# A 3x3 convolution with row transforms: outputs over the pair's own input, and all loads ahead of all stores

## The chip, the cores and the metric

The kernel runs on one core of one Trainium2 chip. The metric is device time in microseconds of one execution; lower is better. The core has five engines with instruction streams of their own: TensorE (PE, with weight loads shown as PEld), VectorE (DVE), ScalarE (ACT), GpSimd (POOL) and SyncE (SP), which here only issues transfers. Transfers between HBM and the on-chip memory SBUF run on 16 DMA engines; matrix products land in PSUM.

## The reference

`x` is 16 images of 64 channels of 64 x 64, `weight` is 128 x 64 x 3 x 3, all float32. Each output is the sum over 64 input channels and nine taps of a zero-padded 3 x 3 convolution:

```
x_pad = np.pad(x, ((0, 0), (0, 0), (1, 1), (1, 1)), mode='constant')
output[b, co] += weight[co, ci, kh, kw] * x_pad[b, ci, kh:kh+h, kw:kw+w]
```

The output has 16 x 128 x 64 x 64 float32, 33.55 MB; the input 16.8 MB and the weights 0.3 MB.

## The kernel before, in words

**Tiling.** Two images make a pair: their 2 x 64 channels fill the 128 partitions, and there are eight pairs. One image plane of 64 x 64 float32 per partition, 2.1 MB over 128 partitions, is a *home*. The tile `homes` has nine of them. `X_HOME` says in which home the input of each pair lands, `O_HOME` in which two neighbouring homes its output is made (two images of 128 output channels, so an output takes two homes). Homes are used again: the inputs of pairs 5, 6 and 7 go where earlier inputs were.

**Work on a half.** Each pair is worked in two halves of 32 output rows. In each half 16 rows (F block) are made with a Winograd-like row transform and 16 rows (G block) with shared products, each 2 x 8 row pairs. GpSimd makes three float16 tiles from the input: `sums` (L106, tile `ss`), `diffs` (L113, `dd`) and `outers` (L119, `ee`); ScalarE makes a fourth, the cast `xh` (L124). In the first half of pair 0 VectorE does GpSimd's part. The transforms of half n + 2 are recorded ahead of the work on half n. TensorE then multiplies (L162) with seven prepared weight matrices into four PSUM accumulators, which are all of PSUM that there is: `pf1`, `pg1`, `pf2`, `pg2`. After a first round, `pf1`, `pg1` and `pf2` hold products that two output rows share. ScalarE copies each to SBUF (`copied`, L182, tiles `ux`, `ug`, `uy` from a pool of four), and TensorE adds a second round onto the same accumulators. The output rows are then sums: VectorE's L231 (`pg2 + ug`), L232 (`pf1 + uy`) and L233 (`ux - pf2`), and ScalarE's copy of `pg1` (L234). All four write rows of every second row of the pair's output homes.

**Order.** `keep` fixes the order on each engine as written. ScalarE's order in a half is: three copies, the cast for the next half, the copy of `pg1`. A half issues 54 products on TensorE.

**Transfers.** At the start SyncE issues the weights (L58), pair 0 in two parts, pairs 1 and 2 (L63), and pairs 3 and 4 in one transfer of 4 MB (L72). `NEXT_LOADS` issues the inputs of pairs 5, 6 and 7 after the first halves of pairs 2, 3 and 4, so they stand between stores on SyncE and wait until the home is free. `store` writes a pair in one transfer of 4 MB where the pair is in `BOTH` (L192), else in two of 2 MB (L201). Pair 0's store is issued on ScalarE's queue (q10 in the profile), all else on SyncE's (q1). `FEW` cuts the second store of pair 5: its last seven rows go as 124 partitions and 4 partitions, beside 128 partitions for the rows ahead.

Of the kernel before, what the change touches and what calls it, by code (L numbers as in the profile page):

```python
# [8 lines left out]
F32 = mybir.dt.float32  # L9
F16 = mybir.dt.float16  # L10
# [5 lines left out]
def kernel(  # L16
# [12 lines left out]
    nc = tc.nc  # L29
    B, CI, H, W = x.shape  # L30
    CO = weight.shape[0]
    assert H == 64 and W == 64 and CI == 64 and CO == 128 and B == 16
    NP = B // 2
    RB = 8

    keep = tc.keep_in_program_order
    x_rows = x.rearrange("b c h w -> (b c) h w")
    w_flat = weight.rearrange("co ci kh kw -> co (ci kh kw)")

    const = ctx.enter_context(tc.tile_pool(name="const", bufs=1))  # L40
    psum = ctx.enter_context(tc.tile_pool(name="psum", bufs=4, space=bass.MemoryType.PSUM))
    slots = ctx.enter_context(tc.tile_pool(name="slots", bufs=1))
    tpool = ctx.enter_context(tc.tile_pool(name="tpool", bufs=4))
    cpool = ctx.enter_context(tc.tile_pool(name="cpool", bufs=3))
    upool = ctx.enter_context(tc.tile_pool(name="upool", bufs=4))

    X_HOME = [0, 1, 2, 7, 8, 2, 7, 8]
    O_HOME = [5, 3, 0, 5, 3, 0, 5, 2]  # L50
    BOTH = (0, 3, 6)
    FEW = 5, 1, 7
    NEXT_LOADS = {(2, 0): 5, (3, 0): 6, (4, 0): 7}
    homes = slots.tile([128, 9, H, W], F32)
    xs = [homes[:, k, :, :] for k in X_HOME]

    w_raw = const.tile([CO, CI * 9], F32)
    keep(nc.sync.dma_start(w_raw, w_flat))  # L58

    def load(p, cuts=((0, H),)):  # L60
        for lo, hi in cuts:
            keep(
                nc.sync.dma_start(  # L63
                    xs[p][:, lo:hi, :], x_rows[128 * p : 128 * p + 128, lo:hi, :]
                )
            )

    load(0, ((0, 34), (34, H)))
    load(1)
    load(2)  # L70
    rows = x_rows[128 * 3 : 128 * 5, :, :].rearrange("(g p) h w -> p g h w", g=2)
    keep(nc.sync.dma_start(homes[:, 7:9, :, :], rows))  # L72

    ident = const.tile([128, 128], F16)
    make_identity(nc, ident)

    w16 = const.tile([CO, 2, CI * 9], F16)
    keep(nc.gpsimd.tensor_copy(w16[:, 0, :], w_raw))  # L78
    keep(nc.scalar.copy(w16[:, 1, :], w_raw))  # L79

    G0, G1, G2, G21, G01, HP, HM = range(7)
    Wt = const.tile([128, 7, 3, CO], F16)
    g0h = const.tile([128, 3 * CO], F32)
    th = const.tile([128, 3 * CO], F32)

    def wrow(i):
        return Wt[:, i, :, :].rearrange("p t c -> p (t c)")
# [10 lines left out]
    F_BLK, G_BLK = (1, 2), (0, 3)  # L98
# [10 lines left out]
    def diffs(eng, p, h):  # L109
# [3 lines left out]
        keep(eng.tensor_sub(t, v[:, j : j + RB, 1, :], v[:, j : j + RB, 0, :]))  # L113
        return t

    def outers(eng, p, h):
        t = tpool.tile([128, 16, W], F16, tag="ee", name="ee")
        r = 16 * F_BLK[h]
        keep(eng.tensor_sub(t, xs[p][:, r - 1 : r + 15, :], xs[p][:, r + 1 : r + 17, :]))  # L119
        return t  # L120

    def cast(p, h):
        t = cpool.tile([128, 17, W], F16, tag="xh", name="xh")
        keep(nc.scalar.copy(t, xs[p][:, C_ROW[h] : C_ROW[h] + 17, :]))  # L124
        return t

    def transforms(eng, p, h):
        return sums(eng, p, h), diffs(eng, p, h), outers(eng, p, h)
# [12 lines left out]
    keep(nc.scalar.copy(wrow(G2), wps[2]))  # L141
    keep(nc.vector.tensor_sub(wrow(G21), wps[2], wrow(G1)))
    tr[0, 0] = s0, d0, outers(nc.vector, 0, 0)
    tr[0, 1] = transforms(nc.gpsimd, 0, 1)

    def mms(tiles, terms, start, stop):
        n = 3 * len(terms)
        i = 0
        for wi, src, row in terms:
            for kw in (1, 0, 2):  # L150
                c_lo, c_hi = max(0, 1 - kw), min(W, W + 1 - kw)
                lo, hi = 0, RB
                at, step, rows = row
                while at + step * lo < 0:
                    lo += 1
                while at + step * (hi - 1) > rows - 1:
                    hi -= 1
                first, last = at + step * lo, at + step * (hi - 1)
                for b2 in range(2):
                    p0 = 64 * b2  # L160
                    keep(
                        nc.tensor.matmul(  # L162
                            tiles[:, b2, lo:hi, c_lo:c_hi],
                            Wt[p0 : p0 + 64, wi, kw, :],
                            src[
                                p0 : p0 + 64,
                                first : last + 1 : step,
                                c_lo + kw - 1 : c_hi + kw - 1,
                            ],
                            start=start and i == 0,  # L170
                            stop=stop and i == n - 1,
                            skip_group_check=not start,
                        )
                    )
                i += 1

    def acc():
        return psum.tile([128, 2, RB, W], F32, tag="acc", name="acc")

    def copied(tiles):  # L180
        ut = upool.tile([128, 2, RB, W], F32, tag="ut", name="ut")
        keep(nc.scalar.copy(ut, tiles))  # L182
        return ut

    halves = [(p, h) for p in range(NP) for h in range(2)]

    def store(p, both):
        if p in BOTH:
            pair = out[2 * p : 2 * p + 2, :, :, :].rearrange("b c h w -> c b h w")

            eng = nc.scalar if p == 0 else nc.sync
            keep(eng.dma_start(pair, both))  # L192
            return
        for b2 in range(2):
            parts = [(0, CO, 0, H)]
            if (p, b2) == FEW[:2]:
                at = H - FEW[2]
                parts = [(0, CO, 0, at), (0, 124, at, H), (124, 4, at, H)]
            for c, n, lo, hi in parts:
                keep(  # L200
                    nc.sync.dma_start(  # L201
                        out[2 * p + b2, c : c + n, lo:hi, :], both[c : c + n, b2, lo:hi, :]
                    )
                )

    for n, (p, h) in enumerate(halves):
        if n + 2 < len(halves):
            tr[halves[n + 2]] = transforms(nc.gpsimd, *halves[n + 2])
        if h == 0:
            both = homes[:, O_HOME[p] : O_HOME[p] + 2, :, :]  # L210
            ov = both.rearrange("p b (j i) c -> p b j i c", i=2)
        ss, dd, ee = tr.pop((p, h))
        xc = xh.pop((p, h))
        jf, jg = RB * F_BLK[h], RB * G_BLK[h]
        sf, sg = jf - 16 * h, jg - 16 * h
        g_at = 2 * jg - C_ROW[h]

        pf1, pg1, pf2, pg2 = acc(), acc(), acc(), acc()
        mms(pf1, [(HP, ss, (sf, 1, 16))], True, True)
        ux = copied(pf1)  # L220
        mms(pg1, [(G1, ss, (sg, 1, 16))], True, True)
        ug = copied(pg1)
        mms(pf2, [(HM, dd, (0, 1, RB))], True, True)
        uy = copied(pf2)
        if n + 1 < len(halves):
            xh[halves[n + 1]] = cast(*halves[n + 1])
        mms(pg2, [(G01, xc, (g_at, 2, 17)), (G2, xc, (g_at + 2, 2, 17))], True, True)
        mms(pf1, [(G0, ee, (0, 2, 16))], False, True)
        mms(pg1, [(G21, xc, (g_at + 1, 2, 17)), (G0, xc, (g_at - 1, 2, 17))], False, True)
        mms(pf2, [(G2, ee, (1, 2, 16))], False, True)  # L230
        keep(nc.vector.tensor_add(ov[:, :, jg : jg + RB, 1, :], pg2, ug))  # L231
        keep(nc.vector.tensor_add(ov[:, :, jf : jf + RB, 0, :], pf1, uy))  # L232
        keep(nc.vector.tensor_sub(ov[:, :, jf : jf + RB, 1, :], ux, pf2))  # L233
        keep(nc.scalar.copy(ov[:, :, jg : jg + RB, 0, :], pg1))  # L234
        if h == 1:
            store(p, both)
        if (p, h) in NEXT_LOADS:
            load(NEXT_LOADS[p, h])


# [28 lines left out]
```

## Time and profile before

| what | value |
|---|---|
| median of the three runs shown | 126.89 us (126.59 to 128.24) |
| the profiled execution's own time | 126.95 us |
| its span, first to last instruction | 125.2 us |
| TensorE busy | 95.7 us, 76% |
| GpSimd busy | 90.5 us, 72% |
| ScalarE busy | 81.4 us, 65% |
| VectorE busy | 63.9 us, 51% |
| read from HBM / written | 17.07 MB / 33.55 MB |

The page cuts the span into 40 slices and shows each engine's busy share of a slice in tenths. The row DMA is the mean busy share of the 16 DMA engines, GB/s what they moved. In rows such as `102.66 1.22 DVE homes L233` the columns are start, duration, engine, tile and line. In rows of groups, `x48 | 45.7, 1020 | 6.3 <-PE` is the count, then the busy time in us and the mean ns of one, then the idle time ahead of them and what ended it. In a table of stretches each row has the stretch, its length, the busy time and count of each engine, the granted TensorE clock, the DMA share and GB/s. SPq and ACTq are the issuing sides of SyncE and ScalarE.

### The profile page before, as it was taken

How to read it: one execution, taken by the hardware profiler on the slowest of the kernel's cores; microseconds unless marked ns; L12 is line 12 of the kernel's file. 1: busy time of each engine (PE TensorE's matmuls, PEld its weight loads, DVE VectorE, ACT ScalarE, POOL GpSimd, SP SyncE). 2: the span in 40 equal slices, each digit the busy share in tenths (PEclk: the TensorE clock that was granted, in tenths of full speed). 3: DMA queues.
4: the chain of work that ended last, by engine and by line, in shares of the span. 5: the costliest groups of instructions: out<-in, count | busy, mean ns of one | idle time of the engine just before them, and what ended most of it. 6: DMA issues, size and time to landing. Idle time of an engine off the chain costs nothing.

```text
span 125.2 us, 2157 instructions
## 1 busy us (share of the span) xinstructions
PE 95.7 (76%) x873; PEld 50.5 (40%) x873; DVE 63.9 (51%) x56; ACT 81.4 (65%) x86; POOL 90.5 (72%) x52
## 2 busy tenths in 40 slices
PE   0349999999999999999999999999999980000000
PEld 0224455455555555555555555555555530000000
DVE  0199657374939375674839393746647392000000
ACT  4457598599797978889897979788897940000000
POOL 2209999999999999999999999999999400000000
PEclk9999999999999999999999999999999997555555
DMA  4999999999999999999999999999999999999981
GB/s 125 375 454 424 429 429 429 435 335 419 424 429 435 435 419 429 403 437 440 437 411 382 440 424 419 429 440 424 435 419 431 426 414 436 429 440 435 419 372 58
DMA packets 3826, 50.77 MB, mean 406 GB/s; under 512 B 360, under 2 KB 488, under 8 KB 744
## 3 DMA queue, kind: packets, MB, share of 16 engines
q1 hardware_dynamic: 3544, 46.43, 88.6%
q10 hardware_dynamic: 272, 4.19, 7.9%
q8 instruction: 7, 0.11, 0.3%
q14 instruction: 3, 0.02, 0.0%
HBM read 17.07 MB, written 33.55 MB: 405 GB/s over the span
## 4 chain that ended last, share of the span: by engine, by line
PE 76%; DVE 3%; DMA 2%; POOL 1%; ACT 0%; issue 0%; DVEq 0%
PE acc L162 76%; DMA w_raw<-in_weight_dram 2%; DVE homes L233 1%; DVE ss L106 1%; POOL w L78 1%; DVE th L133 0%; DVE Wt L134 0%; PE wp L95 0%; ACT g0h L131 0%; DVEq L134 0%
## 5 line engine op out<-in xcount | busy, mean ns | idle before, releaser
L162 PEld LDWEIGHTS <-Wt 64*128 64x128 f16 x864 | 49.6, 96 | 47.0 <-issue 3.7
L182 ACT COPY ut<-acc 128x1024 f32<-128x1024 f32 x48 | 45.7, 1020 | 6.3 <-PE acc L162 6.3
L162 PE MATMUL acc<-xh,Wt 64*128 64x504 f16 (+3 forms) x384 | 46.3, 372 | 0.0
L106 POOL TENSOR_TENSOR ss<-homes 128x1024 f16<-128x1024 f32 x15 | 35.5, 2369 | 4.7 <-DMA homes<-in_x_dram 4.7
L231 DVE TENSOR_TENSOR homes<-acc,ut 128x1024 f32<-128x1024 f32 x16 | 19.6, 1225 | 32.2 <-PE acc L162 29.7
L119 POOL TENSOR_TENSOR ee<-homes 128x1024 f16<-128x1024 f32 x15 | 35.6, 2375 | 0.0
L162 PE MATMUL acc<-ss,Wt 64*128 64x504 f16 (+1 forms) x192 | 24.9, 392 | 2.3 <-DVE ss L106 2.3
L162 PE MATMUL acc<-ee,Wt 64*128 64x504 f16 (+1 forms) x192 | 26.5, 377 | 0.0
L234 ACT COPY homes<-acc 128x1024 f32<-128x1024 f32 x16 | 16.2, 1015 | 11.3 <-PE acc L162 10.7
L233 DVE TENSOR_TENSOR homes<-ut,acc 128x1024 f32<-128x1024 f32 x16 | 19.5, 1220 | 2.0 <-PE acc L162 1.4
L113 POOL TENSOR_TENSOR dd<-homes 128x512 f16<-128x512 f32 x15 | 20.2, 1347 | 0.0
L232 DVE TENSOR_TENSOR homes<-acc,ut 128x1024 f32<-128x1024 f32 x16 | 19.4, 1215 | 0.0
L124 ACT CAST xh<-homes 128x1088 f16<-128x1088 f32 x16 | 17.9, 1120 | 0.0
L162 PE MATMUL acc<-dd,Wt 64*128 64x504 f16 (+1 forms) x96 | 13.9, 392 | 0.0
L95 PE MATMUL wp<-ident,w 128*128 128x128 f16 x9 | 1.1, 309 | 4.6 <-POOL w L78 4.6
L133 DVE SCALAR_TENSOR_TENSOR th<-wp,g0h 128x384 f32<-128x384 f32 x1 | 0.6, 557 | 5.7 <-ACT g0h L131 5.7
L95 PEld LDWEIGHTS <-w 128*128 128x128 f16 x9 | 0.9, 158 | 4.6 <-POOL w L78 4.6
L119 DVE TENSOR_TENSOR ee<-homes 128x1024 f16<-128x1024 f32 x1 | 2.6, 2622 | 0.0
L78 POOL CAST w<-w_raw 128x576 f16<-128x576 f32 x1 | 0.7, 662 | 2.5 <-DMA w_raw<-in_weight_dram 2.5
L79 ACT CAST w<-w_raw 128x576 f16<-128x576 f32 x1 | 0.7, 672 | 1.8 <-DMA w_raw<-in_weight_dram 1.8
L79 ACT ACT_TABLE_LOAD x1 | 1.3, 1283 | 0.7 <-PEq L253 0.7
L106 DVE TENSOR_TENSOR ss<-homes 128x1024 f16<-128x1024 f32 x1 | 1.2, 1216 | 0.0
(15 smaller groups left out, 5.7 us busy)
## 6 DMA issues: line engine op xcount, KB each, us to landing
out_dram<-homes SPq DMA_DIRECT2D x9, 2048.0 KB, 17.5
homes<-in_x_dram SPq DMA_DIRECT2D x5, 2048.0 KB, 18.8
out_dram<-homes SPq DMA_DIRECT2D x2, 4096.0 KB, 22.2
homes<-in_x_dram SPq DMA_DIRECT2D x1, 4096.0 KB, 30.4
out_dram<-homes ACTq DMA_DIRECT2D x1, 4096.0 KB, 18.6
out_dram<-homes SPq DMA_DIRECT2D x1, 1824.0 KB, 23.6
homes<-in_x_dram SPq DMA_DIRECT2D x1, 1088.0 KB, 5.5
homes<-in_x_dram SPq DMA_DIRECT2D x1, 960.0 KB, 7.4
```

Of the source, the lines that this page charges most:

```text
L79: keep(nc.scalar.copy(w16[:, 1, :], w_raw))
L95: keep(nc.tensor.matmul(wps[kh][:, k * CO : k * CO + CO], w16[:, :, 3 * kh + k :: 9], ident))
L106: keep(eng.tensor_add(t, v[:, j : j + 16, 0, :], v[:, j : j + 16, 1, :]))
L113: keep(eng.tensor_sub(t, v[:, j : j + RB, 1, :], v[:, j : j + RB, 0, :]))
L119: keep(eng.tensor_sub(t, xs[p][:, r - 1 : r + 15, :], xs[p][:, r + 1 : r + 17, :]))
L124: keep(nc.scalar.copy(t, xs[p][:, C_ROW[h] : C_ROW[h] + 17, :]))
L162: nc.tensor.matmul(tiles[:, b2, lo:hi, c_lo:c_hi], Wt[p0 : p0 + 64, wi, kw, :], src[p0 : p0 + 64, first : last + 1 : step, c_lo + kw - 1 : ...
L182: keep(nc.scalar.copy(ut, tiles))
L231: keep(nc.vector.tensor_add(ov[:, :, jg : jg + RB, 1, :], pg2, ug))
L232: keep(nc.vector.tensor_add(ov[:, :, jf : jf + RB, 0, :], pf1, uy))
L233: keep(nc.vector.tensor_sub(ov[:, :, jf : jf + RB, 1, :], ux, pf2))
L234: keep(nc.scalar.copy(ov[:, :, jg : jg + RB, 0, :], pg1))
```

## The change

There are eleven homes instead of nine, and each pair's input has one of its own, so that all eight inputs are loaded at the start, ahead of every store on SyncE; `NEXT_LOADS` and the double load of pairs 3 and 4 are gone. A pair's output goes into the home of its own input and one more (`E_HOME`), which need not be neighbours. `E_HOME` uses home 4 for pairs 0, 3 and 7, home 5 for pairs 1 and 5, home 6 for pairs 2 and 6 and home 0, pair 0's own, for pair 4. The shared products are copied straight to the output rows where their sum is going to stand, and VectorE adds in place; the pool of `ut` tiles is gone. As a copy now overwrites input rows, `outers` reads 17 rows in the first half and 15 in the second, into one tile for both halves. The scratch of the weight preparation (`w_raw`, `w16`, `ident`, `g0h`, `th`) lies in home 6 before pair 2's output needs it. Pair 0's store is issued on SyncE in two parts, home 4 first; the pairs stored in one transfer are 1, 2, 4 and 6. TensorE's products keep number, shape and order.

```diff
+    epool = ctx.enter_context(tc.tile_pool(name="epool", bufs=2))
     cpool = ctx.enter_context(tc.tile_pool(name="cpool", bufs=3))
-    upool = ctx.enter_context(tc.tile_pool(name="upool", bufs=4))
-    X_HOME = [0, 1, 2, 7, 8, 2, 7, 8]
-    O_HOME = [5, 3, 0, 5, 3, 0, 5, 2]
-    BOTH = (0, 3, 6)
+    X_HOME = [0, 1, 2, 3, 7, 8, 9, 10]
+    E_HOME = [4, 5, 6, 4, 0, 5, 6, 4]
+    BOTH = (1, 2, 4, 6)
     FEW = 5, 1, 7
-    NEXT_LOADS = {(2, 0): 5, (3, 0): 6, (4, 0): 7}
-    homes = slots.tile([128, 9, H, W], F32)
+    homes = slots.tile([128, 11, H, W], F32)
...
+    def out_homes(p):
+        lo, hi = sorted((X_HOME[p], E_HOME[p]))
+        return homes[:, lo : hi + 1 : hi - lo, :, :]
+
+    spare = homes[:, E_HOME[2], :, :].rearrange("p h w -> p (h w)")
...
     load(0, ((0, 34), (34, H)))
-    load(1)
-    load(2)
-    rows = x_rows[128 * 3 : 128 * 5, :, :].rearrange("(g p) h w -> p g h w", g=2)
-    keep(nc.sync.dma_start(homes[:, 7:9, :, :], rows))
+    for p in range(1, NP):
+        load(p)
...
+    ees = {}
+
     def outers(eng, p, h):
-        t = tpool.tile([128, 16, W], F16, tag="ee", name="ee")
-        r = 16 * F_BLK[h]
-        keep(eng.tensor_sub(t, xs[p][:, r - 1 : r + 15, :], xs[p][:, r + 1 : r + 17, :]))
-        return t
+        if h == 0:
+            ees[p] = epool.tile([128, 32, W], F16, tag="ee", name="ee")
+        lo, hi = (16, 33) if h == 0 else (33, 48)
+        keep(
+            eng.tensor_sub(
+                ees[p][:, lo - 16 : hi - 16, :],
+                xs[p][:, lo - 1 : hi - 1, :],
+                xs[p][:, lo + 1 : hi + 1, :],
+            )
+        )
+        return ees[p]
...
         if p in BOTH:
             pair = out[2 * p : 2 * p + 2, :, :, :].rearrange("b c h w -> c b h w")
-
-            eng = nc.scalar if p == 0 else nc.sync
-            keep(eng.dma_start(pair, both))
+            keep(nc.sync.dma_start(pair, both))
             return
-        for b2 in range(2):
+
+        for b2 in (1, 0) if p == 0 else (0, 1):
...
-            both = homes[:, O_HOME[p] : O_HOME[p] + 2, :, :]
+            both = out_homes(p)
...
+        f0, f1 = (ov[:, :, jf : jf + RB, i, :] for i in range(2))
+        g0, g1 = (ov[:, :, jg : jg + RB, i, :] for i in range(2))
         pf1, pg1, pf2, pg2 = acc(), acc(), acc(), acc()
         mms(pf1, [(HP, ss, (sf, 1, 16))], True, True)
-        ux = copied(pf1)
+        keep(nc.scalar.copy(f1, pf1))
         mms(pg1, [(G1, ss, (sg, 1, 16))], True, True)
-        ug = copied(pg1)
+        keep(nc.scalar.copy(g1, pg1))
         mms(pf2, [(HM, dd, (0, 1, RB))], True, True)
-        uy = copied(pf2)
+        keep(nc.scalar.copy(f0, pf2))
...
-        keep(nc.vector.tensor_add(ov[:, :, jg : jg + RB, 1, :], pg2, ug))
-        keep(nc.vector.tensor_add(ov[:, :, jf : jf + RB, 0, :], pf1, uy))
-        keep(nc.vector.tensor_sub(ov[:, :, jf : jf + RB, 1, :], ux, pf2))
-        keep(nc.scalar.copy(ov[:, :, jg : jg + RB, 0, :], pg1))
+        keep(nc.vector.tensor_add(g1, pg2, g1))
+        keep(nc.vector.tensor_add(f0, pf1, f0))
+        keep(nc.vector.tensor_sub(f1, f1, pf2))
+        keep(nc.scalar.copy(g0, pg1))
         if h == 1:
             store(p, both)
-        if (p, h) in NEXT_LOADS:
-            load(NEXT_LOADS[p, h])
```

More of the change, by code (lines that the diff above doesn't have):

```diff
@@ L43, with spared @@
     tpool = ctx.enter_context(tc.tile_pool(name="tpool", bufs=4))
+    epool = ctx.enter_context(tc.tile_pool(name="epool", bufs=2))
     cpool = ctx.enter_context(tc.tile_pool(name="cpool", bufs=3))
-    upool = ctx.enter_context(tc.tile_pool(name="upool", bufs=4))
-    X_HOME = [0, 1, 2, 7, 8, 2, 7, 8]
-    O_HOME = [5, 3, 0, 5, 3, 0, 5, 2]
-    BOTH = (0, 3, 6)
+    X_HOME = [0, 1, 2, 3, 7, 8, 9, 10]
+    E_HOME = [4, 5, 6, 4, 0, 5, 6, 4]
+    BOTH = (1, 2, 4, 6)
     FEW = 5, 1, 7
-    NEXT_LOADS = {(2, 0): 5, (3, 0): 6, (4, 0): 7}
-    homes = slots.tile([128, 9, H, W], F32)
+    homes = slots.tile([128, 11, H, W], F32)
     xs = [homes[:, k, :, :] for k in X_HOME]
-    w_raw = const.tile([CO, CI * 9], F32)
+    def out_homes(p):
+        lo, hi = sorted((X_HOME[p], E_HOME[p]))
+        return homes[:, lo : hi + 1 : hi - lo, :, :]
+    spare = homes[:, E_HOME[2], :, :].rearrange("p h w -> p (h w)")
+    def spared(at, n):
+        return spare[:, at : at + n]
+    w_raw = spared(0, CI * 9)
     keep(nc.sync.dma_start(w_raw, w_flat))
@@ L68 @@
     load(0, ((0, 34), (34, H)))
-    load(1)
-    load(2)
-    rows = x_rows[128 * 3 : 128 * 5, :, :].rearrange("(g p) h w -> p g h w", g=2)
-    keep(nc.sync.dma_start(homes[:, 7:9, :, :], rows))
-    ident = const.tile([128, 128], F16)
+    for p in range(1, NP):
+        load(p)
+    ident = spared(1920, 64).bitcast(F16)
     make_identity(nc, ident)
-    w16 = const.tile([CO, 2, CI * 9], F16)
+    w16 = spared(576, 576).bitcast(F16).rearrange("p (b k) -> p b k", b=2)
     keep(nc.gpsimd.tensor_copy(w16[:, 0, :], w_raw))
@@ L82 @@
     Wt = const.tile([128, 7, 3, CO], F16)
-    g0h = const.tile([128, 3 * CO], F32)
-    th = const.tile([128, 3 * CO], F32)
+    g0h = spared(1152, 3 * CO)
+    th = spared(1536, 3 * CO)
     def wrow(i):
@@ L178, in acc @@
         return psum.tile([128, 2, RB, W], F32, tag="acc", name="acc")
[L180 to L183, printed above, removed]
     halves = [(p, h) for p in range(NP) for h in range(2)]
@@ L227 @@
         mms(pg2, [(G01, xc, (g_at, 2, 17)), (G2, xc, (g_at + 2, 2, 17))], True, True)
-        mms(pf1, [(G0, ee, (0, 2, 16))], False, True)
+        mms(pf1, [(G0, ee, (16 * h, 2, 32))], False, True)
         mms(pg1, [(G21, xc, (g_at + 1, 2, 17)), (G0, xc, (g_at - 1, 2, 17))], False, True)
-        mms(pf2, [(G2, ee, (1, 2, 16))], False, True)
-        keep(nc.vector.tensor_add(ov[:, :, jg : jg + RB, 1, :], pg2, ug))
-        keep(nc.vector.tensor_add(ov[:, :, jf : jf + RB, 0, :], pf1, uy))
-        keep(nc.vector.tensor_sub(ov[:, :, jf : jf + RB, 1, :], ux, pf2))
-        keep(nc.scalar.copy(ov[:, :, jg : jg + RB, 0, :], pg1))
+        mms(pf2, [(G2, ee, (16 * h + 1, 2, 32))], False, True)
+        keep(nc.vector.tensor_add(g1, pg2, g1))
+        keep(nc.vector.tensor_add(f0, pf1, f0))
+        keep(nc.vector.tensor_sub(f1, f1, pf2))
+        keep(nc.scalar.copy(g0, pg1))
         if h == 1:
             store(p, both)
-        if (p, h) in NEXT_LOADS:
-            load(NEXT_LOADS[p, h])
 _INS = ['x', 'weight']
```

## The prediction

> **What bounds the kernel now.** I read the page's slices first, then the chain, then a table of stretches, then the tail.
>
> ```profile
> span 125.2 us, 2157 instructions
> PE   0349999999999999999999999999999980000000
> DMA  4999999999999999999999999999999999999981
> GB/s 125 375 454 424 429 429 429 435 335 419 424 429 435 435 419 429 403 437 440 437 411 382 440 424 419 429 440 424 435 419 431 426 414 436 429 440 435 419 372 58
> q1 hardware_dynamic: 3544, 46.43, 88.6%
> q10 hardware_dynamic: 272, 4.19, 7.9%
> HBM read 17.07 MB, written 33.55 MB: 405 GB/s over the span
> 102.66 1.22 DVE homes L233
> ```
>
> TensorE is full until slice 32 and then idle: computing ends at 102.66 + 1.22 = 103.9 us. The DMA row is full from the second slice to the last but two. The chain of waits gives TensorE 76% of the span, but its last piece is this VectorE instruction; what follows, 21 us of stores alone, is not in it. So the bound is the stream of 50.6 MB through the 16 DMA engines (q1 and q10 together, 96.5% of the span), and computing matters only where it feeds that stream late. The question is how much of the stream is lost. A table of stretches gives it (the last two columns are the DMA share and GB/s):
>
> ```profile
> core 0: us, PE busy (x) PEld busy (x) DVE busy (x) ACT busy (x) POOL busy (x), PEclk, DMA share, GB/s
> 0.00:3.00 3.00, 0.00 (x0) 0.00 (x0) 0.00 (x0) 1.28 (x1) 0.70 (x6) 1.00 0.44 114
> 3.00:6.00 3.00, 1.15 (x9) 0.92 (x9) 0.32 (x1) 1.52 (x3) 0.66 (x1) 1.00 0.98 374
> 6.00:24.00 18.00, 15.91 (x130) 7.70 (x132) 13.62 (x14) 11.98 (x15) 14.86 (x7) 1.00 1.02 432
> 24.00:30.00 6.00, 6.00 (x58) 3.16 (x56) 3.48 (x3) 6.00 (x7) 6.00 (x4) 1.00 1.00 380
> 30.00:45.00 15.00, 15.00 (x144) 8.11 (x142) 9.51 (x8) 12.52 (x14) 15.00 (x9) 1.00 1.01 429
> 45.00:60.00 15.00, 15.00 (x144) 8.02 (x141) 8.45 (x8) 12.97 (x15) 15.00 (x9) 1.00 1.00 424
> 63.00:69.00 6.00, 6.00 (x59) 3.20 (x57) 3.82 (x4) 5.07 (x6) 6.00 (x5) 1.00 1.00 406
> 69.00:84.00 15.00, 15.00 (x144) 8.04 (x142) 8.57 (x8) 13.20 (x14) 15.00 (x8) 1.00 1.01 429
> 84.00:99.00 15.00, 15.00 (x144) 8.08 (x142) 9.67 (x9) 12.30 (x14) 14.25 (x8) 1.00 1.01 428
> 99.00:102.00 3.00, 3.00 (x32) 1.60 (x28) 1.86 (x2) 1.40 (x2) 0.00 (x0) 1.00 0.97 413
> 105.00:120.00 15.00, 0.00 (x0) 0.00 (x0) 0.00 (x0) 0.00 (x0) 0.00 (x0) 0.50 1.01 434
> ```
>
> Only loads move in 6 to 24 us (432 GB/s), only stores in 105 to 120 us (434). So neither direction is slower by itself. Against 432, a stretch of T us at g GB/s loses T x (432 - g)/432: 0.72 us in 24 to 30, 0.10 in 30 to 45, 0.28 in 45 to 60, 0.36 in 63 to 69, 0.10 in 69 to 84, 0.14 in 84 to 99, 0.13 in 99 to 102. Together 1.83 us. The share column stays at 1.00 there: the engines are not without work, their packets take longer.
>
> Which transfers lie there? The SyncE queue's issues in order, and the landings:
>
> ```profile
> 34.92 1.17 SPq L201 DMA_DIRECT2D out_dram<-homes  x2
> 39.56 0.34 SPq L63 DMA_DIRECT2D homes<-in_x_dram  x1
> 46.40 0.81 SPq L201 DMA_DIRECT2D out_dram<-homes  x2
> 51.32 0.34 SPq L63 DMA_DIRECT2D homes<-in_x_dram  x1
> 57.92 0.38 SPq L192 DMA_DIRECT2D out_dram<-homes  x1
> 63.07 0.35 SPq L63 DMA_DIRECT2D homes<-in_x_dram  x1
> 23.33 0.42 ACTq L192 DMA_DIRECT2D out_dram<-homes  x1
> DMA to landing us min/median/max: 10.1/19.5/25.5
> ```
>
> The last row is that of L201's twelve stores; its shortest fits pair 1's first: 34.9 + 10.1 = 45.0. A transfer of 2.1 MB takes 4.85 us at 432 GB/s; in queue order pair 1's second store then ends at 49.9, load 5 at 54.7, pair 2 at 64.4, load 6 at 69.3, pair 3 at 79.0, load 7 at 83.8. So the dips at 45 to 60 and 63 to 69 are where loads 5 and 6 stand between stores, load 7's stretch is nearly clean, and the deepest dip, 24 to 30, is where the first five loads give way to the first store.
>
> **The change, part by part.**
>
> *Loads ahead of all stores (eight homes, NEXT_LOADS gone).* The bytes and the number of transfers hardly change: x3 and x4 go as two loads instead of one. On SyncE the nine issues, each of about the 0.34 us of the rows above, are over a few us after the start; the last two also wait for the weights and x0's first part, both among the first to land. Removed are three turns from stores to a load and back. Price: at most 0.28 + 0.36 + 0.10 = 0.74 us gained; at least nothing, since the dips are placed there by bytes and not by a packet's name. One turn from loads to stores stays, the 0.72 us of 24 to 30, now at about 42 us; between 0 and 0.72 of it could go, as in the new order the stores stand queued long before. I take 0.7 gained for the three and nothing for the one.
>
> *Pair 0's store from ScalarE's queue to SyncE's.* It passes all loads. By the first rows 0.34 + 1.12 + 7.78 = 9.24 MB had moved at 24 us; the remaining 7.83 of the 17.07 MB of loads take 18.1 us: loads end at 42.2. Then, 4.85 us each, pair 0's halves end at 47.0 and 51.9 and the pairs follow every 9.7 us: 61.6, 71.3, 81.0, 90.7, 100.4, 110.1. By the issues above pairs 0 to 3 are computed by 23.3, 34.9, 46.4 and 57.9, and so on every 11.5 us to 103.9: each is 19 to 6 us early for its turn, so the stream never starves. The 0.42 us of issue leaves ScalarE; it is hidden work and counts nothing.
>
> *The shared products go into the output's homes.* Copies onto `ut` become copies of the same 128x1024 into strided rows, and VectorE's second operand is strided too:
>
> ```profile
> L182 ACT COPY ut<-acc 128x1024 f32<-128x1024 f32 x48 | 45.7, 1020 | 6.3 <-PE acc L162 6.3
> L234 ACT COPY homes<-acc 128x1024 f32<-128x1024 f32 x16 | 16.2, 1015 | 11.3 <-PE acc L162 10.7
> 9.95 2.62 DVE L119 TENSOR_TENSOR ee<-homes 128x1024 f16<-128x1024 f32 x1
> 9.59 1.01 ACT L182 COPY ut<-acc 128x1024 f32<-128x1024 f32 x1 [0.80 <-PE acc L162]
> 45.76 2.84 ACT L182 COPY ut<-acc 128x1024 f32<-128x1024 f32 x3 [0.23 <-PE acc L162]
> 97.56 2.84 ACT L182 COPY ut<-acc 128x1024 f32<-128x1024 f32 x3 [0.24 <-PE acc L162]
> 48.14 0.83 PE L162 MATMUL acc<-ee,Wt 64*128 64x512 f16 x6
> 95.87 2.38 POOL L119 TENSOR_TENSOR ee<-homes 128x1024 f16<-128x1024 f32 x1
> ```
>
> Copying into the homes costs 1015 ns against 1020: nothing. VectorE's sums should keep the 1.22 us of L233 above; the other bound is the 2.62 us of its `outers` (two operands from SBUF, one for the sums as before), so I take 1.22. What is new are waits of the first copy of a half, and behind it on ScalarE stand the other two copies, the cast for the next half and the copy of `pg1`; TensorE's second round on `pf1` waits for it:
> - It overwrites rows of the input, so it waits for `outers`. In the first half that is VectorE's, grown from 1024 to 1088 columns: 9.95 + 2.62 x 17/16 = 12.7 instead of 9.6. The second round on `pf1` then comes at about 13.8, some 0.3 us late. In later halves it is GpSimd's: the last ends at 98.25, the copy stood at 97.56, so 0.7 us late at worst. (The halves now take 17 and 15 rows, 32 together as before.)
> - Pair 3 needs home 4, which pair 0's first store must have left. It ends at 47.0, up to 47.7 if the turn costs its 0.72, and lands about 1.2 us later (the last packets end before 124, the span at 125.2): 48.2 to 48.9, against a copy at 45.76. ScalarE stands 2.4 to 3.1 us; TensorE's round at 48.14 comes at about 49.9, 1.8 us late. Of pairs 4 to 7 each needs a home that comes free 3 us or more before (pair 4: home 0 at 53.1 to 53.8, its copy at 45.76 + 11.5 = 57.3).
>
> Together computing ends some 2 to 3 us later, at about 106 to 107, and pair 7's turn at the stream comes at 110 to 111. Cost: nothing, the backlog of stores covers it. Without that backlog all of it would be paid.
>
> *Weights' scratch in a home, epool, blank lines:* no further instruction, no wait on the path; nothing.
>
> *The tail.* The engines do not end together:
>
> ```profile
> 120.00:121.00 1.00, 0.00 (x0) 0.00 (x0) 0.00 (x0) 0.00 (x0) 0.00 (x0) 0.50 0.77 328
> 121.00:122.00 1.00, 0.00 (x0) 0.00 (x0) 0.00 (x0) 0.00 (x0) 0.00 (x0) 0.50 0.69 295
> 122.00:123.00 1.00, 0.00 (x0) 0.00 (x0) 0.00 (x0) 0.00 (x0) 0.00 (x0) 0.50 0.42 180
> 123.00:124.00 1.00, 0.00 (x0) 0.00 (x0) 0.00 (x0) 0.00 (x0) 0.00 (x0) 0.50 0.04 16
> ```
>
> Their mean end is 120 + 0.77 + 0.69 + 0.42 + 0.04 = 121.9, the last just under 124: the slowest is 2 us behind the mean. Nothing in the change evens them or makes them more uneven that I can see. I take the 2 us as they are; which engine gets the slow packets may move it by 1 us to either side.
>
> **Sum.** The profiled execution took 126.95 us (span 125.2, 1.75 around it); the median of the runs shown is 126.89, the same for this purpose. 126.95 - 0.7 = 126.25, say 126.2.
>
> **The rivals.**
> - *The stream has no more to give.* The dips may be packets that would be slow in any order, as 99 to 102 us is (413 GB/s, no load near). Then the time is 126.9. For it: the dips are small and 428 to 429 is all that long stretches of stores reach. Against it: 432 and 434 in the unmixed stretches. The Trainium skill, "DMA: Bandwidth & Descriptors", section Measured, gives 425 GB/s for one 16 MB load by a single core; were that a ceiling, the mixed stretches at 424 to 429 would be at it already and the change would gain nothing. This trace passes it (432, 434), so I give this rival a fifth.
> - *All of the loss goes, and the tail too.* One turn, with stores long queued, costs nothing, and half of the 2 us of tail goes with the even order: 126.95 - 1.83 - 1.0 = 124.1. Against it: the turn at 24 to 30 cost 0.72 and will still be made; nothing in the change evens the engines.
> - *Home 4 becomes the bound.* Pair 3's first copy waits for pair 0's store, now behind all loads. Up to a wait of about 7 us nothing is paid (pair 7 is 6 us early for its turn, TensorE has 1.3 us from the copy's end, 45.76 + 1.0, to its round at 48.14). Beyond, each us is paid in full; over 2% slower starts at a wait of 10 us, a landing at 56. If home 4 came free only with pair 1's stores, at 62 to 63, the wait would be 17 us and the time 126.2 + 10 = 136. Against it: the queue order by bytes gives 48 to 49, and pair 0's half with home 4 goes first.
>
> **How the numbers follow.** Forecast 0.70 (its own range 125.5 to 126.8: 0 to 1.46 us of turns gone), no gain 0.18, the large gain 0.06, home 4 0.06. The range 125.0 to 127.4 holds the first two with the tail's 1 us; it leaves the last two out. 2%, about what a measurement of this kernel can tell from no change, is 124.35 to 129.4: faster 0.07 (the large gain and a lucky tail), slower 0.05 (most of the home 4 case), within 0.88.
>
> **What would show it.** Right: GB/s at 430 or more from 6 to 42 us with no dip at 25, one dip at about 42, then no dip at 48 to 55 or 64 to 70; SyncE's first store issued near 24 and landing near 48; a ScalarE wait on a DMA of 2 to 3 us at pair 3's first copy and no other over 1 us; computing's end at 105 to 107. Wrong: a slice under 400 after 45 us while computing still runs (a starved stream), a VectorE end after 110, or a tail that leaves the last engine more than 3 us behind the mean.

## The result and the profile after

The changed kernel took 126.39 us in the median of 22 runs (126.18 to 126.84), the kernel before on the same chip 126.77 us (126.42 to 128.27). The ratio is 0.9961 with a 95% interval of 0.9943 to 0.9979: 0.4% faster, a small gain that is clear of noise and well within 2%. Some executions take over 1.5% longer than the fastest of their kernel, and the ratios leave those out. The forecast was 126.2 us with a range of 125.0 to 127.4. The profiled execution took 126.42 us with a span of 124.6. A second measurement, run e9 below, gave 0.9952 (0.9928 to 0.9976).

The slices of the changed kernel, from its page:

```profile
span 124.6 us, 2133 instructions
PE   0349699999999996499999999999999999500000
PEclk9999999999999999859999999999999999965555
GB/s 122 382 448 436 431 426 426 426 426 426 436 421 436 326 431 447 415 436 431 423 426 421 429 442 434 426 421 431 421 421 434 431 419 436 421 421 431 436 379 63
q1 hardware_dynamic: 3816, 50.63, 96.5%
q8 instruction: 7, 0.11, 0.3%
```

Before, the GB/s row dipped to 335 in its ninth slice (25 to 28 us), to 403 in its seventeenth and to 411 and 382 in its slices 21 and 22. Now it is flat until the fourteenth slice, has one dip to 326 there (40.5 to 43.6 us), and is flat again. TensorE has a hole that it did not have, in slices 16 and 17 (and a small one in slice 5), and ends two slices later. A table of stretches of the same run sizes both (last columns: granted clock, DMA share, GB/s):

```profile
24.00:30.00 6.00, 6.00 (x60) 3.20 (x58) 3.57 (x3) 5.08 (x7) 6.00 (x4) 1.00 1.00 429
39.00:42.00 3.00, 3.00 (x30) 1.59 (x28) 2.10 (x2) 2.41 (x3) 3.00 (x3) 1.00 1.00 366
42.00:45.00 3.00, 3.00 (x31) 1.60 (x29) 1.86 (x2) 2.46 (x4) 3.00 (x2) 1.00 1.00 404
45.00:60.00 15.00, 12.32 (x100) 5.81 (x98) 5.96 (x6) 9.07 (x10) 15.00 (x9) 0.89 1.00 427
63.00:69.00 6.00, 6.00 (x59) 3.02 (x56) 3.44 (x3) 5.06 (x6) 6.00 (x4) 1.00 1.02 434
105.00:120.00 15.00, 2.79 (x27) 1.25 (x22) 3.58 (x3) 1.70 (x2) 0.00 (x0) 0.67 1.01 429
```

The dip at 24 to 30 us is gone (380 before, 429 now) and stands at 39 to 45 us; the one at 63 to 69 us is gone (406 before, 434 now); 45 to 60 us went only from 424 to 427. A row counts each packet where it starts, so a row of 6 us is good to some 10 GB/s only: shifted to 62 to 68 us it reads 403 before and 423 now. By the prediction's formula the one turn left costs 3 x (432 - 366)/432 + 3 x (432 - 404)/432 = 0.65 us, against 0.72 before.

The hole in TensorE is pair 3's wait. In the timeline (start, duration, then in brackets the idle time ahead and what ended it):

```profile
50.45 1.01 ACT L235 COPY homes<-acc 128x1024 f32<-128x1024 f32 x1 [4.45 <-DMA out_dram<-homes]
51.51 0.95 PE L180 MATMUL acc<-ee,Wt 64*128 64x512 f16 x6 [2.68 <-ACT homes L235]
109.11 1.69 SPq L213 DMA_DIRECT2D out_dram<-homes  x2
```

ScalarE stood 4.45 us until pair 0's store had left home 4, TensorE 2.68 us behind it. The last pair's stores were issued at 109.1, when computing ended, instead of 104 before. Yet the stream ran at 429 GB/s over 105 to 120 us: it never went dry.

### The profile page after: what moved, and what is told of

Same layout as the page of the kernel before. It is cut to its first block, busy times and chain, and to the rows that moved or that the text cites. A ratio compares the mean times of both kernels' runs of the same rounds, so it can differ in the third digit from the quotient of the medians.

```text
span 124.6 us, 2133 instructions
## 1 busy us (share of the span) xinstructions
PE 97.2 (78%) x873; PEld 50.5 (41%) x873; DVE 64.0 (51%) x56; ACT 81.2 (65%) x86; POOL 90.4 (73%) x52
## 4 chain that ended last, share of the span: by engine, by line
PE 52%; DMA 24%; DVE 8%; ACT 2%; issue 1%; POOL 1%; ACTq 0%; SPq 0%; DVEq 0%
PE acc L180 51%; DMA out_dram<-homes 21%; DMA homes<-in_weight_dram 2%; DVE ee L132 2%; DVE homes L248 2%; DVE ss L114 1%; ACT homes L235 1%; ACT homes L237 1%; POOL homes L86 1%; DVE dd L121 0%; DVE homes L151 0%; DVE Wt L152 0%; PE wp L103 0%; ACT homes L149 0%; DVE Wt L158 0%
## 5 line engine op out<-in xcount | busy, mean ns | idle before, releaser
L180 PE MATMUL acc<-xh,Wt 64*128 64x504 f16 (+3 forms) x384 | 47.1, 377 | 0.1
L246 DVE TENSOR_TENSOR homes<-acc,homes 128x1024 f32<-128x1024 f32 x16 | 19.6, 1225 | 37.3 <-PE acc L180 26.3
L132 POOL TENSOR_TENSOR ee<-homes 128x960 f16<-128x960 f32 (+1 forms) x15 | 35.8, 2389 | 0.0
L235 ACT COPY homes<-acc 128x1024 f32<-128x1024 f32 x16 | 16.2, 1012 | 13.6 <-PE acc L180 5.0
L249 ACT COPY homes<-acc 128x1024 f32<-128x1024 f32 x16 | 16.2, 1015 | 9.4 <-PE acc L180 9.4
L248 DVE TENSOR_TENSOR homes<-homes,acc 128x1024 f32<-128x1024 f32 x16 | 19.5, 1220 | 2.0 <-PE acc L180 1.2
L247 DVE TENSOR_TENSOR homes<-acc,homes 128x1024 f32<-128x1024 f32 x16 | 19.4, 1214 | 0.0
L239 ACT COPY homes<-acc 128x1024 f32<-128x1024 f32 x16 | 16.5, 1032 | 0.0
L237 ACT COPY homes<-acc 128x1024 f32<-128x1024 f32 x16 | 16.3, 1018 | 0.0
L103 PE MATMUL wp<-homes 128*128 128x128 f16 x9 | 1.1, 309 | 4.6 <-POOL homes L86 4.6
L132 DVE TENSOR_TENSOR ee<-homes 128x1088 f16<-128x1088 f32 x1 | 2.8, 2806 | 0.0
L103 PEld LDWEIGHTS <-homes 128*128 128x128 f16 x9 | 0.9, 158 | 4.5 <-POOL homes L86 4.5
L86 POOL CAST homes<-homes 128x576 f16<-128x576 f32 x1 | 0.7, 662 | 2.5 <-DMA homes<-in_weight_dram 2.5
L87 ACT CAST homes<-homes 128x576 f16<-128x576 f32 x1 | 0.7, 671 | 1.7 <-DMA homes<-in_weight_dram 1.7
```

The lines of the kernel that those rows point to most:

```text
L132: eng.tensor_sub(ees[p][:, lo - 16 : hi - 16, :], xs[p][:, lo - 1 : hi - 1, :], xs[p][:, lo + 1 : hi + 1, :],)
L180: nc.tensor.matmul(tiles[:, b2, lo:hi, c_lo:c_hi], Wt[p0 : p0 + 64, wi, kw, :], src[p0 : p0 + 64, first : last + 1 : step, c_lo + kw - 1 : ...
L235: keep(nc.scalar.copy(f1, pf1))
L237: keep(nc.scalar.copy(g1, pg1))
L239: keep(nc.scalar.copy(f0, pf2))
L246: keep(nc.vector.tensor_add(g1, pg2, g1))
```

## The experiments

The theory after the result: the stream of transfers sets the time; each turn from stores to a load and back costs it some tenths of a us, and three such turns are gone; computing, which now ends 5 us later, is just covered. The rivals: the gain comes from the single queue or from the homes; the wait at pair 3 costs something; the tail decides.

**Loads back between the stores (e2, repeated as e10 beside the changed kernel as e9).** Each input keeps its own home; only the place of three loads changes.

```diff
+    NEXT_LOADS = {(2, 0): 5, (3, 0): 6, (4, 0): 7}
...
-    for p in range(1, NP):
+    for p in range(1, 5):
         load(p)
...
         if h == 1:
             store(p, both)
+        if (p, h) in NEXT_LOADS:
+            load(NEXT_LOADS[p, h])
```

Expected of e2:

> The changed kernel, but loads 5, 6 and 7 stand again where they stood before, behind the stores of pairs 1, 2 and 3 on SyncE; every input keeps its own home. Theory (each turn from stores to a load and back slows some packets): dips near 48 to 55 and 64 to 70 us are back, the time is 126.7 to 126.9, 0.3 to 0.5 above the changed kernel, although home 4 lands 14 us earlier, pair 3 does not wait and computing ends near 104. Rival (the 0.4 us came from the single queue or from the homes, not from the order of loads and stores): 126.3 to 126.5. Second rival (computing's wait at pair 3 costs time in the changed kernel): the time falls below 126.3.

Of e9:

> The changed kernel itself, beside e10_late_loads_again on one chip, so that the two can be compared directly: 126.3 to 126.6, 0.3 to 0.5 below the kernel before.

Of e10:

> e2_late_loads once more: the changed kernel with loads 5, 6 and 7 behind the stores of pairs 1, 2 and 3. Theory (three turns of the stream, 0.1 to 0.3 us each): 0.4 to 0.9 us above e9_changed_again. Rival (the first measurement was off): equal to it within 0.2.

Measured: e2 127.29 us, 1.0025 of the kernel before (0.9995 to 1.0054). On one chip with the same runs of before, e9 126.34 us, 0.9952 (0.9928 to 0.9976), and e10 127.26 us, 1.0036 (1.0015 to 1.0056). The two intervals don't meet: the order of loads and stores alone is worth 0.92 us in the medians. In e10 pair 3 has no wait and computing ends at 104.6, and still it is the slower one, so the wait at pair 3 is not what counts. Its stretches show the dips back in place; the last three rows are its tail:

```profile
24.00:30.00 6.00, 6.00 (x59) 3.18 (x56) 3.57 (x3) 5.08 (x6) 6.00 (x4) 1.00 0.98 382
45.00:60.00 15.00, 15.00 (x144) 7.96 (x142) 9.01 (x8) 12.75 (x14) 15.00 (x9) 1.00 1.00 420
63.00:69.00 6.00, 6.00 (x58) 3.17 (x56) 4.11 (x5) 5.07 (x6) 6.00 (x4) 1.00 1.02 419
120.00:121.00 1.00, 0.00 (x0) 0.00 (x0) 0.00 (x0) 0.00 (x0) 0.00 (x0) 0.50 0.80 344
121.00:122.00 1.00, 0.00 (x0) 0.00 (x0) 0.00 (x0) 0.00 (x0) 0.00 (x0) 0.50 0.69 295
122.00:123.00 1.00, 0.00 (x0) 0.00 (x0) 0.00 (x0) 0.00 (x0) 0.00 (x0) 0.50 0.39 164
```

Added up as in the prediction, the DMA engines of e10 end at 120 + 0.80 + 0.69 + 0.39 = 121.88 us in the mean. In e9 the shares are 0.77, 0.61 and 0.16, which gives 121.54. So these two profiled executions, each the shortest of its runs, show only 0.34 of the 0.92 us as time of the stream. The rest would have to lie in how far the slowest engine stands behind the mean in a usual execution, which neither trace shows.

One thing stays open: e10 has the turns of the kernel before, but is 0.47 us above it (e2: 0.3). In the mean its engines end when those of the kernel before do (121.88 against 121.92), so in this execution the stream pays nothing for the other edits. At 126.53 us it was the shortest of its runs, so the trace doesn't show what the median has more.

**One queue in the kernel before (e8).**

```diff
-            eng = nc.scalar if p == 0 else nc.sync
+            eng = nc.sync
```

> The kernel before with pair 0's store issued on SyncE instead of ScalarE's queue, nothing else. Theory (the gain came from the order of loads and stores): 126.7 to 127.0, as before; the dip at 24 to 30 us stays. Rival (two queues side by side made the deep dip at 24 to 30 us): the dip is gone and the time is 126.2 to 126.5.

Measured: 126.78 us, 1.0001 of the kernel before (0.9973 to 1.0030). Moving pair 0's store to SyncE gains nothing. (The profiled execution, of 128.44 us, was the longest of its runs; still the dip stands where it stood, 371 GB/s over 24 to 30 us.) Two queues side by side don't make it.

**The transfers alone (e5, e6, e11).** All computing is left out; the same bytes go in and out in three orders. e5 has all loads ahead, e6 three of them behind stores, e11 six.

```diff
-    for p in range(1, NP):
+    for p in range(1, 5):
         load(p)
...
+    for p in range(NP):
+        store(p, out_homes(p))
+        if p in (1, 2, 3):
+            load(p + 4)
```

(This is e6; e5 has the loop without its last two lines and loads as the changed kernel; e11 loads pair 1 ahead and pair p + 2 behind each of the first six stores.)

Expected of e5:

> Leaves out all computing: the transfers of the changed kernel alone, in its order (nine loads, then all stores of the two homes of each pair; the three homes without an input are filled with zeros), so every store can be issued as soon as its load has landed. Theory (the stream is the bound, computing costs it nothing): 125.9 to 126.4, within 0.5 us of the changed kernel's 126.39. Rival (computing's traffic or its late stores cost the stream something): 125.5 or less.

Of e6:

> Leaves out all computing: the same transfers, but loads 5, 6 and 7 behind the stores of pairs 1, 2 and 3, as before the change. Theory (turns between stores and loads cost the stream): 0.3 to 0.7 us above e5_stream_ahead, with the dips at loads 5, 6 and 7. Rival (the dips need computing beside them, or the second queue): equal to e5_stream_ahead within 0.2 us.

Of e11:

> Leaves out all computing: the same transfers with only pairs 0 and 1 loaded ahead and each further load behind a store, so that the stream turns from stores to a load and back six times instead of three (e6_stream_between) or none (e5_stream_ahead). Theory (each turn costs the same, the 0.95 us between those two being three turns): 127.3 to 127.7. Rival (what costs is that loads stand late, not how often the stream turns): 126.4 to 126.7, as e6_stream_between.

Measured: e5 125.6 us, 0.9912 of the kernel before (0.9877 to 0.9947); e6 126.55 us, 0.9956 (0.9928 to 0.9984); e11 1.0106 (1.0055 to 1.0157), by three runs of 127.22, 128.58 and 128.79 us (its other three took 129.2 to 131.8). More turns, more time, without any computing beside it: 0.95 us for three turns in the medians, 0.6 by the ratios, and the intervals of e5 and e6 overlap. From 120 us on the shares of e5 are the two in the rows below, those of e6 0.69, 0.35, 0.23 and 0.04, those of e11 0.99, 0.39, 0.27 and 0.12: the engines end at about 120.6, 121.3 and 121.8 us in the mean, in the order of the turns. e11 confirms the direction, but scatters too much to say that each turn costs the same; two of its three runs lie above its range. Stretches of e5 and then e6 (the columns are length, GpSimd busy, clock, DMA share, GB/s):

```profile
24.00:30.00 6.00, 0.00 (x0) 1.00 1.02 434
36.00:45.00 9.00, 0.00 (x0) 1.00 1.00 410
45.00:60.00 15.00, 0.00 (x0) 1.00 1.01 435
63.00:69.00 6.00, 0.00 (x0) 1.00 1.01 431
120.00:121.00 1.00, 0.00 (x0) 1.00 0.27 115
121.00:122.00 1.00, 0.00 (x0) 1.00 0.31 131
```

```profile
24.00:30.00 6.00, 0.00 (x0) 1.00 1.02 377
36.00:45.00 9.00, 0.00 (x0) 1.00 1.00 428
45.00:60.00 15.00, 0.00 (x0) 1.00 1.01 428
63.00:69.00 6.00, 0.00 (x0) 1.00 1.02 421
```

The dips follow the order of the transfers with nothing else running. e5 is also a floor: the changed kernel stands 0.8 us above its own transfers, which was neither the theory's 0 to 0.5 nor the rival's 0.9 or more.

**Home 4 freed later (e1), and earlier (e7).** In e1 pair 0's two stores change places; in e7 the store of home 4 is cut, so that the 32 rows that pair 3's first half needs go first.

```diff
-        for b2 in (1, 0) if p == 0 else (0, 1):
+        for b2 in range(2):
```

```diff
             parts = [(0, CO, 0, H)]
+            if (p, b2) == (0, 1):
+                parts = [(0, CO, 0, 32), (0, CO, 32, H)]
```

Expected of e1:

> Pair 0's two stores change places: home 0 first, home 4 second. Home 4 then lands one transfer of 4.9 us later, at about 55.2 instead of 50.35, and pair 3's first copy waits 9.3 us instead of 4.45. Theory (computing is hidden only by the backlog of stores, and of the 6 us of slack that stood before the change some 1.5 are left, as computing already ends at 109.1): computing ends at about 114, the stream runs dry for about 3 us near 113 to 116, and the time is 129 to 130 us. Rival (the stream is the bound whatever computing does, its backlog is larger than I reckon): computing ends at about 114, the time stays at 126.4 to 126.8.

Of e7:

> The changed kernel with pair 0's store of home 4 cut at row 32, the first 32 rows first. Pair 3's first half needs only those; they land about 2.4 us earlier, near 48, so the first copy waits about 2 us instead of 4.45, TensorE idles 0.3 us instead of 2.7, keeps its full clock, and computing ends near 106 instead of 109.1. Theory (the wait is hidden by the backlog): the time stays at the changed kernel's, 126.3 to 126.6. Rival (the wait at pair 3 costs): 125.7 or less.

Measured: e1 128.67 us, 1.0142 of the kernel before (1.0088 to 1.0197); e7 126.46 us, 0.9968 (0.9934 to 1.0001). First e1's rows, of its timeline and then of its stretches, after them e7's in the same order:

```profile
55.41 1.01 ACT L235 COPY homes<-acc 128x1024 f32<-128x1024 f32 x1 [9.09 <-DMA out_dram<-homes]
113.64 1.22 DVE L248 TENSOR_TENSOR homes<-homes,acc 128x1024 f32<-128x1024 f32 x1
```

```profile
102.00:105.00 3.00, 3.00 (x32) 1.56 (x30) 1.28 (x2) 2.67 (x4) 0.00 (x0) 1.00 0.55 150
114.00:117.00 3.00, 0.00 (x0) 0.00 (x0) 0.86 (x1) 0.01 (x1) 0.00 (x0) 0.91 0.58 240
```

```profile
47.45 1.01 ACT L237 COPY homes<-acc 128x1024 f32<-128x1024 f32 x1 [1.29 <-DMA out_dram<-homes]
103.37 1.22 DVE L250 TENSOR_TENSOR homes<-homes,acc 128x1024 f32<-128x1024 f32 x1
```

```profile
45.00:60.00 15.00, 15.00 (x144) 8.12 (x142) 8.94 (x8) 12.63 (x14) 15.00 (x9) 1.00 1.03 436
```

With a wait of 9.09 us computing ends at 114.9 and the stream runs dry twice: ahead of pair 6's store, issued at 103.4, it falls to 150 GB/s for 3 us, ahead of pair 7's to 240, and by the formula 2.0 and 1.3 us are lost there. The time rises by 2.3 us over the changed kernel in the medians, and by 2.8 us between the profiled executions (129.25 and 126.42 us). The direction is the theory's; the median lies just below its 129 to 130, and it had one dry stretch where there are two. With a wait of 1.29 us computing ends at 104.6, 4.5 us earlier than in the changed kernel, and the time doesn't move. So up to the changed kernel's 109.1 the end of computing costs nothing, and 5.8 us more cost 2.3 to 2.8: some 3.0 to 3.5 us were left, if each us beyond is paid in full.

**The uneven split of pair 5's store (e3, e4, e12).** Four rows instead of seven, none, and six on top of e7.

```diff
-    FEW = 5, 1, 7
+    FEW = 5, 1, 4
```

Expected of e3:

> The changed kernel with 4 instead of 7 rows in the unevenly split end of pair 5's store. Theory on the tail (the 31-row shares of that piece put some 1.8 us more on four DMA engines than the others, and these four now end last, about 0.7 us behind the next): the four end 0.9 us earlier, the other twelve 0.2 later; the last engine ends near 122.8 instead of 123.3 and the time is 125.9 to 126.1. Rival (which engine ends last is chance, the split doesn't set it): 126.3 to 126.5.

Of e4:

> The changed kernel with pair 5's second store in one even piece. Theory on the tail: the four engines end 1.8 us earlier and the other twelve 0.5 later, so that one of the twelve ends last, near 123.2; time 126.1 to 126.4, between e3_few4 and the changed kernel. Rival (chance): 126.3 to 126.5. A third view (the split saves what it was put there for): 126.9 or more.

Of e12:

> e7_home4_rows_first with six instead of seven rows in the uneven end of pair 5's store: the four engines that end last in the changed kernel end some 0.3 us earlier. 126.1 to 126.4 if the split sets the tail; 126.4 to 126.6 if which engine ends last changes from run to run anyway.

Measured: e3 126.56 us, 0.9967 (0.9932 to 1.0003); e4 126.97 us, 0.9998 (0.9968 to 1.0027); e12 126.57 us, 0.9978 (0.9961 to 0.9994). My theory of the tail fell: four rows gain nothing, and none loses about 0.5 us, as the third view of e4 had it. In e4's profiled execution the shares from 120 to 124 us are 0.69, 0.39, 0.15 and 0.04: the mean end, 121.3 us, is earlier than the changed kernel's 121.6, but some engine still works after 123. Without computing (e5, above) the share from 120 to 122 us is 0.27 and 0.31, four to five engines of 16 working alone, which fits the four that the split loads. In the full kernel the shares there are higher, so others end late as well. No version here that computes is faster than the changed kernel.

## Why the prediction was right

- *The three turns, 0.7 us.* The mechanism holds (e9 against e10, e5 against e6). The size stays open: 0.9 us in the medians, 0.34 us in the mean end of the engines. Of the three stretches that lie behind the 0.7, 63 to 69 us shows it (434 for 406, or 423 for 403 a us earlier), 45 to 60 hardly, and load 7's stretch, 69 to 84 us, went from 429 to 426. The prediction measured the loss against 432 GB/s, which the stores beside computing don't reach over long stretches even in the new order (426 over 69 to 84 us, 431 over 84 to 99). Against 428 the three stretches before lose 0.14 + 0.31 + 0 = 0.45 us.
- *The turn that stays, 0.72 us and moved to 42 us.* 0.65 us at 39 to 45 (0.33 in e7, whose first store is cut in two: 408 GB/s over these 6 us).
- *Moving pair 0's store to SyncE costs nothing.* e8: 1.0001.
- *All other edits cost nothing.* This is where the net gain came out at 0.4 rather than 0.7 us. In the medians the order is worth 0.9 us, the whole change 0.4 to 0.45, and e10, which has all the edits but the order, is 0.3 to 0.5 us above the kernel before. Which edit it is was not separated; what remains between e8 and e10 are the two loads in place of a double one, other pairs stored in one transfer, and the homes with the work in place. So it is partly luck that the forecast came this near: a gain that was larger in the medians met a cost that was put at nothing.
- *Copies and sums keep their lengths.* They do, in the page's groups, and the first copy waits for VectorE's `outers` until 12.80, where 12.7 was forecast (last row, of the timeline):

```profile
L235 ACT COPY homes<-acc 128x1024 f32<-128x1024 f32 x16 | 16.2, 1012 | 13.6 <-PE acc L180 5.0
L237 ACT COPY homes<-acc 128x1024 f32<-128x1024 f32 x16 | 16.3, 1018 | 0.0
L246 DVE TENSOR_TENSOR homes<-acc,homes 128x1024 f32<-128x1024 f32 x16 | 19.6, 1225 | 37.3 <-PE acc L180 26.3
L132 DVE TENSOR_TENSOR ee<-homes 128x1088 f16<-128x1088 f32 x1 | 2.8, 2806 | 0.0
```

```profile
12.80 1.01 ACT L235 COPY homes<-acc 128x1024 f32<-128x1024 f32 x1 [4.07 <-DVE ee L132]
```

- *Home 4, a wait of 2.4 to 3.1 us.* Too short: 4.45. The loads were placed by the mean rate of the engines; if a transfer has landed only when its slowest engine is done, that is too early. The rows of the loads and of L213's stores:

```profile
L73 SPq DMA_DIRECT2D homes<-in_x_dram x9: 327/439/667, 1.2 to 6.8; - x9
DMA to landing us min/median/max: 5.6/25.8/38.7
```

```profile
L213 SPq DMA_DIRECT2D out_dram<-homes x10: 332/653/1285, 23.9 to 109.5; - x10
DMA to landing us min/median/max: 9.8/16.5/26.4
```

The last load was issued at 6.8 and landed 38.7 us later, at 45.5, where I had 42.2 for its bytes; pair 0's first store, issued at 23.9, landed at 50.3, one transfer of 4.8 us on. The dip and the landing explain about 1.9 of the 3.3 us; that the rest is the slowest engine is argued from the tail, not shown.

- *Computing ends at 106 to 107, pair 7's turn comes at 110 to 111.* It ended at 109.05. Without the wait at pair 3 it ends at 104.6 (e10) against 103.9 before, within the 0.3 and 0.7 us reckoned for the other waits; the rest is the longer wait, and behind it the slow clock described below, which was not reckoned with. That the backlog covers it held, with 3.0 to 3.5 us to spare where 3 to 5 were reckoned, and e1 shows what it costs beyond.
- *The tail stays.* From 120 us the shares are 0.77, 0.58, 0.27 and 0.00:

```profile
120.00:121.00 1.00, 0.00 (x0) 0.00 (x0) 0.00 (x0) 0.00 (x0) 0.00 (x0) 0.50 0.77 328
121.00:122.00 1.00, 0.00 (x0) 0.00 (x0) 0.00 (x0) 0.00 (x0) 0.00 (x0) 0.50 0.58 246
122.00:123.00 1.00, 0.00 (x0) 0.00 (x0) 0.00 (x0) 0.00 (x0) 0.00 (x0) 0.50 0.27 115
```

The mean end is 121.6 against 121.9, which is 0.3 us of the gain seen directly.

Of the rivals, "no more to give" falls with e9 against e10, and "home 4 becomes the bound" was right about the mechanism: e1 shows it, one transfer beyond what the change does. Its threshold of a wait of 7 us comes out of e1 as well, though the prediction's way to it was another. From the changed kernel to e1 the wait grew by 4.64 us and computing's end by 5.81, so each us of wait moved the end by 1.25; the 3.0 to 3.5 us that were left are then 2.4 to 2.8 us of wait beyond 4.45, about 7 in all. The prediction had each us of wait past the first 1.3 move the end by one us, and 6 us of slack. By these runs a us of wait costs more, and the slack is larger, 8.2 to 8.7 us (from 103.9 to 109.1, and 3.0 to 3.5 beyond): the two errors cancel.

## What to carry to other kernels

When the DMA share is at 1.00 from start to end, the busy time of the computing engines decides little (leaving out all computing won 0.8 us of 126 here), and something may be won in the order of the transfers: compare the GB/s of a mixed stretch with that of pure loads and pure stores, and keep loads and stores apart if there is memory for it. A wait put on a computing engine is free only as long as stores are queued behind it; measure that backlog by making the wait longer once and shorter once. Place a landing later than bytes over mean rate: here home 4 came free 3.3 us later, and 1.4 us of that stays unexplained.

## What the runs showed of the hardware

**A short idle halves TensorE's clock.** The row in the result has TensorE idle for 2.68 us; in e9, the same kernel, it was 3.0 us, and the clock fell there too (0.89 over 45 to 60 us in both). These stretches follow, with the granted clock in the third column from the end:

```profile
52.00:54.00 2.00, 2.00 (x12) 0.69 (x10) 1.53 (x2) 2.00 (x3) 2.00 (x2) 0.52 0.94 401
54.00:56.00 2.00, 2.00 (x14) 0.91 (x12) 0.82 (x2) 1.24 (x2) 2.00 (x2) 0.63 1.05 451
56.00:58.00 2.00, 2.00 (x22) 1.02 (x20) 1.22 (x1) 1.28 (x3) 2.00 (x2) 1.00 1.03 442
```

12 and 14 products in 2 us each, where 22 run in the 2 us after them. This is why an idle time of 2.68 us put off the end of computing by more than that: 0.7 us are there without it too (e10 ends at 104.6 against 103.9 before), the idle time cost 2.7, and the rest of the 5.1, some 1.7, is put down to the slow products. In e7, with a wait of 1.29 us, the clock stayed at 1.00 throughout. The Trainium skill, "TensorE: Matmul & The Clock Gate", Part 1, has the half clock come after at least one idle window of about 3.4 us; here less than that sufficed.

**Instructions come as DMA packets beside the stream.** The changed kernel has seven 16 KB packets on the instruction queue (0.11 MB and 0.3% of the 16 engines' time, the q8 row), e5 with 75 instructions has none, and e5 takes 0.8 us less. The Trainium skill, "Runtime: NRT & Kernel Launch", Instruction fetch mechanics, calls the fetch hidden because the sequencers issue more slowly than it refills. That may hold for the engines that run the instructions; no run here shows what the packets cost the other transfers. 0.3% of 124.6 us is some 0.4 us, so spread evenly over the 16 engines they would make half of the 0.8 us. e5 also leaves out all of computing's traffic in SBUF, and the two were not separated.
